# A two-layer streaming encoder on one core: where V's weights are scaled, how output weights are spaced, which engine forms V's left sums, and when layer 2's weight rows are loaded

## The chip, the cores and the metric

The kernel runs on one core of a Trainium2 chip. The core has five engines with a queue each: TensorE (PE) multiplies matrices into PSUM, VectorE (DVE) and ScalarE (ACT) work elementwise on SBUF and PSUM, GpSimd (POOL) works elementwise on SBUF, and SyncE (SP) issues the DMA transfers. Each queue runs in order; engines wait for each other through semaphores. The metric is the device time of one execution in microseconds; the median of several runs is compared.

## The reference

The input x has 2048 rows of 1024 floats. Layer A is a gated MLP, layer B an attention over chunks of 64 rows with K and V made once from the residual stream. All in float32:

```python
h = rms_norm(x, a_norm_g)
u, v, z = split(h @ w_in, 3)                       # each 2048 wide
u, v = gelu(u), layer_norm(gelu(v), ln_g, ln_b)
mixed = einsum('hts,bgshc->bgthc', masked(w_s), v in groups of 128 rows) + b_s
x = x + (u * mixed * silu(z)) @ w_out
k, v = split(rms_norm(x, kv_norm_g) @ w_kv, 2)     # 16 heads of 64
q, z = split(rms_norm(x, b_norm_g) @ w_qz, 2)
# each chunk of 64 rows attends to itself and the 8 chunks before it
p = softmax(q @ k.T / 8 + rel_bias[clipped distance])
x = x + ((p @ v) * silu(z)) @ w_b_out
return rms_norm(x, final_norm_g)
```

## The kernel before

**Split products.** Every large product is made of three matmuls of 128 x 512 (`mm3`, L99): a float32 operand is split into a high part (a rounded copy, made on ACT, L238) and a low part (the difference, made on DVE, L241). Left factors are called S, right factors T.

**Seven products in place of eight.** The products of layer A, the output product "o" and V's product "v" are blocked two by two, and each runs in seven passes, `PH = (1, 2, 6, 5, 7, 4, 3)`, with sums of blocks on the left and right and sums of results on the way out. A pass has eight steps (`NJ`), one for each pair of row blocks; the passes of n = 0, 1 (V of layer A), 2 to 5 (u and z), "o" and "v" make one list of steps, and `start[n, ph]` is the number of a pass's first step. A step has 12 matmuls, in "o" 24.

**The order by hand.** `run_steps` (L443) goes through the steps. In each it runs the events given for it with `at(s, f)`, then flushes what was put off with `later(k, f)` and issues the step's product and its eviction (`act`), prepares the left factor of the step three ahead (`prep`, `LOOK = 3`), and runs the weight work in `ts`. `later(1, f)` called from an event runs f in the same step, since the count is that of the last flush. Weight work is made by `make_t` (L250) and placed by `add_t` (L459): for each quarter (or half) q a load into a tile of the tag "raw" (four buffers), a combination of blocks on POOL (`pieces`, L243), and a finish, the split into T (ACT and DVE). Its offsets `(o, d)` mean step `start + o + d * q`.

**V's and layer 2's weights.** The norm gains are multiplied into the weights once: `load_scaled` (L149) loads a raw tile, multiplies on POOL (L157), and leaves the store of the scaled tile (L160) to the next call, by way of `deferred`. In "o" it is called eight times for V's weights (`wvs`, L888, steps nin + 20 and on, one every three) and three times for layer 2's first rows (L896), where `nin = start["o", 1]`. Layer 2's rows of the first chunk (t = 0) are scaled in place, in `one` (L1087), by `load_split` (L163), which loads, scales, splits and then feeds 24 matmuls; later chunks load the scaled rows from `wk3`.

**Left factors of "o".** `prep_out` (L802) loads blocks of y into the tag "A" (four buffers, `y_load`) and adds or subtracts them on DVE (L812, L815, L820).

**Rows between "o" and "v".** `row_load`, `row_norm` and `row_flip` (L908 to L945) load a finished row block, square it on ACT (into the PSUM tile that its transposes later use), take the power on POOL (L928), scale it on POOL (L930), transpose it on PE (L939) and store it.

**Left factors of "v".** `s7_of_v` (L992) makes s7 = a11 - a21 on POOL and a22 - s7 on DVE (L997), `s4_of_v` (L999) a third difference on POOL. s7 lies in one tile of the tag "hh", which the right factors of V's first pass use before it. `evict` (L346) takes the results out of PSUM; for V's first pass the copy is on DVE (L353), for "o" on ACT (L355). `done_vo` (L1002) splits the results of V (L1009 on ACT, L1010 on POOL).

**Startup.** `block_c` and `block_d` (L509, L519) make the left factors of the second row block of each pair; L724 to L728 place them among the norms of these blocks.

Of the kernel before, what the change touches and what calls it, by code (L numbers as in the profile page):

```python
# [9 lines left out]
F32 = mybir.dt.float32  # L10
# [7 lines left out]
P = 128  # L18
# [15 lines left out]
def trunk_kernel(  # L34
# [113 lines left out]

    def load_scaled(src, name, gain=None, keep=None):  # L149
        while deferred:  # L150
            deferred.pop(0)()
        raw = sh.tile([P, 1024], F32, tag="raw", name=f"raw_{name}", bufs=4)
        nc.sync.dma_start(raw[:], src)
        if gain is not None:
            k = gain.shape[1]
            r3 = raw[:].rearrange("p (k c) -> p k c", k=k)
            nc.gpsimd.tensor_tensor(  # L157
                r3, r3, gain.broadcast_to([P, k, 1024 // k]), op=ALU.mult
            )
            deferred.append(lambda: nc.sync.dma_start(keep, raw[:]))  # L160
        return raw
# [30 lines left out]
    with ExitStack() as actx:  # L192
# [153 lines left out]
        def evict(n, ph, j, ps, done, c22=None):  # L346
# [3 lines left out]
            if ph == 1:  # L350
                xa[n, j] = acc_tile(f"x{n}_{j}")
                if n == "v":
                    nc.vector.tensor_copy(xa[n, j][:], ps[:])  # L353
                else:
                    nc.scalar.copy(xa[n, j][:], ps[:])  # L355
# [103 lines left out]
        def add_t(ts, at, n, ph, src, nq, where, chain_of, offs):  # L459

            tops[n, ph], fs = make_t(n, ph, src, nq, where, chain_of)
            for f_, (o, d) in zip(fs, offs):
                for q in range(nq):
                    s = at + o + d * q
                    ts.setdefault(max(s, -LOOK), []).append(lambda f_=f_, q=q: f_(q))
# [258 lines left out]
        for j in range(NJ):  # L724
            e = j * 7 // 4
            norm_at(e - 1, e, block_b, j)
            at(e + 2, lambda j=j: block_c(j))
# [148 lines left out]
        for i, ph in enumerate(PH):  # L876
# [3 lines left out]
                6: ((-12, 2), (-11, 2), (-7, 1)),  # L880
                4: ((-14, 1), (-13, 1), (-7, 1)),
            }.get(ph, ((-9, 1), (-8, 1), (-7, 1)))
# [5 lines left out]
        for i, (r, c, q) in enumerate(wvs):  # L888
            g = kg[:, 4 * r + 2 * q : 4 * r + 2 * q + 2, :]
            at(  # L890
                nin + 20 + 3 * i,
                lambda r=r, c=c, q=q, g=g: load_scaled(
                    w_vv[r, c, q], f"bv{r}{c}{q}", g, wvs[r, c, q][:]
                ),
            )
        for c in range(3):  # L896
            at(nin + 43 + 2 * c, lambda c=c: load_scaled(*kqz_source(0, 0, c)))


# [16 lines left out]
        def row_norm(blk):  # L916
            xs = xn[blk]
            pool = ptrs[0] if blk // 2 % 2 else nxp[1]
            pt = pool.tile([P, KD, P], F32, tag="tr", name=f"tn{blk}")
            rs = [sm.tile([P, 1], F32, tag="rr", name=f"rn{blk}_{c}", bufs=6) for c in range(2)]  # L920
            for c in range(2):
                nc.scalar.activation(
                    pt[:, 4 * c : 4 * c + 4, :].rearrange("p a b -> p (a b)"), xs[c][:],
                    AF.Square, scale=1.0 / 32, accum_out=rs[c][:],
# [4 lines left out]
            for xt in xs:  # L929
                nc.gpsimd.tensor_scalar(xt[:], xt[:], r[:], 1.0, op0=mul, op1=mul)  # L930
            xn[blk] = xs, pt

        def row_flip(blk):
            t, b = divmod(blk, TB)
            xs, pt = xn.pop(blk)
# [19 lines left out]
        s7 = []  # L955
# [7 lines left out]
        def prep_v(ph, j):  # L963
# [13 lines left out]
            elif ph == 7:  # L977
                v = s7[0][:, j, :]
# [13 lines left out]
        def s7_of_v(j):  # L992
            if j == 0:
                s7.append(sh.tile([P, NJ, 512], F32, tag="hh", name="s7"))
            a, b = x_pair(1, j, "s")
            later(1, lambda: pieces(s7[0][:, j, :], sc[j][0], a, sub))
            later(2, lambda: tv(sc[j][0], b, s7[0][:, j, :], op=sub))  # L997

        def s4_of_v(j):  # L999
            pieces(sc[j][1], sc[j][1], sc[j][0], sub)  # L1000
# [39 lines left out]
        for j in range(NJ):  # L1040
# [4 lines left out]
            at(nv + 5 + 4 * j // 3, lambda j=j: s7_of_v(j))  # L1045
            at(start["v", 6] + 1 + j, lambda j=j: s4_of_v(j))
# [24 lines left out]
    with ExitStack() as bctx:  # L1071
# [15 lines left out]
        def one(t, p, c):  # L1087
            wh, wl = load_split(
                *kqz_source(t or p == 0, p, c)
            )  # L1090
# [424 lines left out]
```

## Time and profile before

| what | value |
|---|---|
| median of 3 runs | 2765.57 us (2763.31 to 2768.7) |
| the profiled execution, from start to end | 2760.59 us |
| its span, first to last instruction | 2758.8 us |
| granted PE clock over the span | 0.987 |
| DVE, ACT, POOL busy | 72%, 47%, 31% |
| DMA over the span | 655.33 MB, mean 238 GB/s |

A line of the profile names an instruction by its line in the kernel, engine, operation, and output <- inputs by tile names without their numbers. "So" is a left factor of "o", "Sv" of "v"; "Po" and "Pv" are their PSUM results; xv, yv, cv and xo are results being summed; "As" and "A" are blocks loaded for the left factors; "tn" holds transposes of normed rows. "SPq" is the DMA queue of SP. "PEld" is the load of weights into PE, which overlaps its matmuls. A matmul's time is a latency: in a full pipeline one starts every 0.23 us and takes 0.39. An arrow in a wait names who ended it.

### The profile page before, as it was taken

Reading aid. Unit: us, or ns where it says so; the run is one execution under the profiler, and the core shown is the slowest. Engines: PE = TensorE matmul, PEld = TensorE weight load, DVE = VectorE, ACT = ScalarE, POOL = GpSimd, SP = SyncE. Lnnn points to the kernel's source line nnn. Section 1 sums busy time; section 2 is a strip of 40 time slices with the busy share of each in tenths; the row PEclk is TensorE's granted clock in tenths of the full one; section 3 lists DMA queues with packets and bytes.
Section 4 is the critical chain, followed back from the end, with each engine's and each line's share of the span. In section 5 each row is a group of like instructions: output and inputs, shape, how many; then the busy total and the mean of one; then the engine's idle time right before and its main releaser. Section 6 shows DMA issues by size and latency. Waiting matters only on the chain.

```text
span 2758.8 us, 38718 instructions
## 1 busy us (share of the span) xinstructions
PE 2658.7 (96%) x13312; PEld 2212.1 (80%) x13312; DVE 1972.8 (72%) x3081; ACT 1300.1 (47%) x2266; POOL 844.3 (31%) x811
## 2 busy tenths in 40 slices
PE   8999999999999999989897999999999999999997
PEld 7788888888888888777676777878888888888886
DVE  5655666676666777856546857778888888878887
ACT  5422242433434343322452545655666566746663
POOL 3511124131321315335537555312221222212221
PEclk9999999999999999999999999999999999999999
DMA  7899999987868777767996787555556555555431
GB/s 285 297 325 340 316 330 328 322 304 236 330 225 301 290 272 288 258 222 272 320 293 199 256 297 249 179 178 159 166 161 207 153 152 157 174 166 165 141 123 61
DMA packets 265636, 655.33 MB, mean 238 GB/s; under 512 B 26465, under 2 KB 71521, under 8 KB 265441
## 3 DMA queue, kind: packets, MB, share of 16 engines
q1 hardware_dynamic: 265440, 652.86, 70.3%
q8 instruction: 106, 1.74, 0.3%
q14 instruction: 90, 0.73, 0.1%
HBM read 501.76 MB, written 140.51 MB: 233 GB/s over the span
## 4 chain that ended last, share of the span: by engine, by line
PE 68%; DVE 11%; DMA 8%; POOL 5%; issue 5%; ACT 2%; SPq 1%; POOLq 0%; DVEq 0%; ACTq 0%
PE P L100 9%; PE P L101 9%; PE P L102 9%; PE pj L100 5%; PE pj L101 5%; PE pj L102 5%; PE s L1187 4%; PE tp L1226 4%; PE pv L1253 3%; DMA A<-ytd 2%; PE bo L102 2%; PE bo L101 2%; PE bo L100 2%; DMA raw_b<-in_w_kqz 1%; DVE pt L1230 1%
## 5 line engine op out<-in xcount | busy, mean ns | idle before, releaser
L100 PE MATMUL P<-T,S 128*128 128x512 f32 x1248 | 497.2, 398 | 2.7 <-ACT S L238 1.7
L101 PE MATMUL P<-T,S 128*128 128x512 f32 x1248 | 488.4, 391 | 0.5 <-DVE T L241 0.5
L102 PE MATMUL P<-T,S 128*128 128x512 f32 x1248 | 488.7, 392 | 0.0
L1206 POOL TENSOR_SCALAR pr<-pr,sl 128x640 f32<-128x640 f32 (+4 forms) x256 | 208.3, 814 | 708.3 <-DVE sl L1205 655.5
L100 PE MATMUL pj<-hh_b,wh_b 128*128 128x512 f32 x768 | 314.5, 410 | 1.2 <-ACT hh_b L136 1.2
L101 PE MATMUL pj<-hl_b,wh_b 128*128 128x512 f32 x768 | 304.5, 396 | 1.1 <-DVE hl_b L137 1.1
L102 PE MATMUL pj<-hh_b,wl_b 128*128 128x512 f32 x768 | 302.8, 394 | 0.0
L102 PEld LDWEIGHTS P<-T,S 128*128 128x128 f32 x1248 | 235.5, 189 | 50.6
L100 PEld LDWEIGHTS P<-T,S 128*128 128x128 f32 x1248 | 235.8, 189 | 47.5 <-ACT S L238 1.9
L101 PEld LDWEIGHTS P<-T,S 128*128 128x128 f32 x1248 | 235.9, 189 | 44.9 <-DVE T L241 0.9
L1202 ACT ACTIVATE pr<-pr,nm 128x640 f32<-128x640 f32 (+4 forms) x256 | 195.6, 764 | 118.3 <-DVE nm L1195 111.0
L1230 DVE TENSOR_TENSOR pt<-tp,pt 128x640 fp32r<-128x640 f32 (+4 forms) x256 | 188.6, 737 | 58.9 <-ACT pt L1229 57.0
L1229 ACT CAST pt<-tp 128x640 fp32r<-128x640 f32 (+4 forms) x256 | 159.2, 622 | 135.9 <-PE tp L1226 134.5
L1195 DVE CUSTOM_DVE_ANT_0 pr<-s,bias 128x640 f32<-128x640 f32 (+4 forms) x256 | 188.0, 734 | 28.1 <-PE s L1187 23.3
L1226 PEld LDWEIGHTS tp<-ident,pr 128*128 128x128 f32 x1120 | 131.7, 140 | 54.6 <-POOL pr L1206 17.4
L1226 PE MATMUL tp<-ident,pr 128*128 128x128 f32 x1120 | 166.0, 274 | 8.5 <-POOL pr L1206 6.1
L102 PEld LDWEIGHTS pj<-hh_b,wl_b 128*128 128x128 f32 x768 | 145.0, 189 | 29.7
L100 PEld LDWEIGHTS pj<-hh_b,wh_b 128*128 128x128 f32 x768 | 145.2, 189 | 19.4 <-ACT hh_b L136 2.8
L101 PEld LDWEIGHTS pj<-hl_b,wh_b 128*128 128x128 f32 x768 | 145.9, 190 | 15.8 <-DVE hl_b L137 2.0
L1253 PE MATMUL pv<-pt,V 128*128 128x256 f32 x960 | 139.6, 285 | 0.0
L169 DVE TENSOR_TENSOR wl_b<-raw_b,wh_b 128x1024 fp32r<-128x1024 f32 x96 | 121.5, 1266 | 24.7 <-ACT wh_b L168 23.2
L168 ACT CAST wh_b<-raw_b 128x1024 fp32r<-128x1024 f32 x96 | 100.5, 1049 | 66.7 <-PE pj L101 37.6
(249 smaller groups left out, 5955.7 us busy)
## 6 DMA issues: line engine op xcount, KB each, us to landing
S<-hsd SPq DMA_DIRECT2D x288, 512.0 KB, 5.2
rw<-in_w_a SPq DMA_DIRECT2D x108, 512.0 KB, 6.0
raw_b<-wk SPq DMA_DIRECT2D x75, 512.0 KB, 4.0
A<-ytd SPq DMA_DIRECT2D x72, 512.0 KB, 5.4
hsd<-S SPq DMA_DIRECT2D x56, 512.0 KB, 3.9
V<-vhd SPq DMA_DIRECT2D x112, 256.0 KB, 4.3
rwo<-in_w_out SPq DMA_DIRECT2D x40, 512.0 KB, 5.0
bias<-reld SPq DMA_DIRECT2D x64, 320.0 KB, 3.0
```

The costliest lines, as they stand in the source:

```text
L100: mm(ps, lh, rh, start=first, stop=False)
L101: mm(ps, lh, rl, start=False, stop=False)
L102: mm(ps, ll, rh, start=False, stop=last)
L169: nc.vector.tensor_tensor(wl[:], raw[:], wh[:].bitcast(F32), op=ALU.subtract)
L1187: mm(ps[:, sg, :w], q[:, qb * P : (qb + 1) * P], kx[:, koff + sg * w : koff + (sg + 1) * w], start=i == 0, stop=i == 1,)
L1195: nc.vector.tensor_tensor_reduce(out=pr[:, c0:].rearrange("p (a b) -> p a b", a=nseg), in0=ps[:, :nseg, :w], in1=bias[:, c0:].rearrange("p ...
L1202: nc.scalar.activation(pr[:, c0:], pr[:, c0:], AF.Exp, scale=-1.0, bias=nm[:], accum_out=sl[:])
L1206: nc.gpsimd.tensor_scalar(pr[:, c0:], pr[:, c0:], sl[:], 1.0, op0=ALU.mult, op1=ALU.mult)
L1226: tpose(tp[:, b, :], pr[:, b * P : (b + 1) * P], ident[:])
L1229: nc.scalar.copy(oh, tp[:, b0:5, :])
L1230: nc.vector.tensor_tensor(pt[:, 1, b0 + qq : 5 + qq, cs], tp[:, b0:5, :], oh.bitcast(F32), op=ALU.subtract)
L1253: mm(po[:, 0, :], keys(i), pt[:, j, i, :], start=(t == 0 and j == 0 and i == blocks[0]), stop=(j == 1 and i == blocks[-1]),)
```

## The change

- **V's weights and layer 2's first rows** are loaded, scaled and stored in the u/z passes: eleven jobs, the first five in n = 5, the next five in n = 4, the last in n = 3, each three steps ahead of a pass. A function of its own, `scaled`, loads in the event, multiplies in the same step's flush and stores two steps later. The calls in "o" are gone.
- **The output weights' quarters** are two steps apart in every pass but the first, with a step each between load, combination and finish. `add_t` now goes quarter by quarter, so within one step the functions of an earlier quarter come first.
- **V's left sums**: s7 and the third difference are formed on DVE; s7 lies in eight tiles of the tag "acc"; s7 begins at nv + 2 in place of nv + 5 (`nv = start["v", 1]`). The copies of V's first pass out of PSUM go from DVE to ACT.
- **Row norms**: the squares are written to a bfloat16 SBUF tile, the scaling is on ACT and put off by `later(1)`, and the PSUM tile is taken in `row_flip`.
- **Layer 2 rows**: after each `load_split` in `one`, the raw tile of the next product (in the order 1, 0, 2 within a pair of heads, then the next pair, then the next chunk) is loaded and kept in `early`.
- **Startup**: all norms are placed before all `block_c` and `block_d`.

```diff
+    early = {}
+    def load_raw(src, name):
+        raw = sh.tile([P, 1024], F32, tag="raw", name=f"raw_{name}", bufs=4)
+        nc.sync.dma_start(raw[:], src)
+        return raw
     def load_scaled(src, name, gain=None, keep=None):
         while deferred:
             deferred.pop(0)()
-        raw = sh.tile([P, 1024], F32, tag="raw", name=f"raw_{name}", bufs=4)
-        nc.sync.dma_start(raw[:], src)
+        raw = early.pop(name, None) or load_raw(src, name)
...
                 xa[n, j] = acc_tile(f"x{n}_{j}")
-                if n == "v":
-                    nc.vector.tensor_copy(xa[n, j][:], ps[:])
-                else:
-                    nc.scalar.copy(xa[n, j][:], ps[:])
+                nc.scalar.copy(xa[n, j][:], ps[:])
...
-            for f_, (o, d) in zip(fs, offs):
-                for q in range(nq):
+            for q in range(nq):
+                for f_, (o, d) in zip(fs, offs):
                     s = at + o + d * q
...
             norm_at(e - 1, e, block_b, j)
+        for j in range(NJ):
+            e = j * 7 // 4
             at(e + 2, lambda j=j: block_c(j))
...
                 1: ((-11, 1), (-9, 1), (-8, 1)),
-                6: ((-12, 2), (-11, 2), (-7, 1)),
-                4: ((-14, 1), (-13, 1), (-7, 1)),
-            }.get(ph, ((-9, 1), (-8, 1), (-7, 1)))
+                6: ((-11, 2), (-10, 2), (-8, 2)),
+            }.get(ph, ((-10, 2), (-9, 2), (-8, 2)))
...
-        for i, (r, c, q) in enumerate(wvs):
-            g = kg[:, 4 * r + 2 * q : 4 * r + 2 * q + 2, :]
-            at(
-                nin + 20 + 3 * i,
-                lambda r=r, c=c, q=q, g=g: load_scaled(
-                    w_vv[r, c, q], f"bv{r}{c}{q}", g, wvs[r, c, q][:]
-                ),
-            )
-        for c in range(3):
-            at(nin + 43 + 2 * c, lambda c=c: load_scaled(*kqz_source(0, 0, c)))
+        def scaled(src, name, gain, keep):
+            raw = sh.tile([P, 1024], F32, tag="raw", name=f"raw_{name}", bufs=4)
+            nc.sync.dma_start(raw[:], src)
+            k = gain.shape[1]
+            r3 = raw[:].rearrange("p (k c) -> p k c", k=k)
+            later(1, lambda: nc.gpsimd.tensor_tensor(
+                r3, r3, gain.broadcast_to([P, k, 1024 // k]), op=mul
+            ))
+            later(3, lambda: nc.sync.dma_start(keep, raw[:]))
+        jobs = [
+            (w_vv[r, c, q], f"bv{r}{c}{q}", kg[:, 4 * r + 2 * q : 4 * r + 2 * q + 2, :],
+             wvs[r, c, q][:])
+            for r, c, q in wvs
+        ] + [kqz_source(0, 0, c) for c in range(3)]
+        for i, job in enumerate(jobs):
+            n, ph = 5 - i // 5, (1, 5, 7, 4, 3)[i % 5]
+            at(start[n, ph] - 3, lambda job=job: scaled(*job))
...
         def row_norm(blk):
             xs = xn[blk]
-            pool = ptrs[0] if blk // 2 % 2 else nxp[1]
-            pt = pool.tile([P, KD, P], F32, tag="tr", name=f"tn{blk}")
+            jk = nxp[0].tile([P, 2, 512], BF16, tag="xv", name=f"jn{blk}", bufs=4)
...
-            for xt in xs:
-                nc.gpsimd.tensor_scalar(xt[:], xt[:], r[:], 1.0, op0=mul, op1=mul)
-            xn[blk] = xs, pt
+            def scale():
+                for xt in xs:
+                    nc.scalar.mul(xt[:], xt[:], r[:])
+            later(1, scale)
...
         def s7_of_v(j):
-            if j == 0:
-                s7.append(sh.tile([P, NJ, 512], F32, tag="hh", name="s7"))
             a, b = x_pair(1, j, "s")
-            later(1, lambda: pieces(s7[0][:, j, :], sc[j][0], a, sub))
-            later(2, lambda: tv(sc[j][0], b, s7[0][:, j, :], op=sub))
+            s7[j] = acc_tile(f"s7_{j}")
+            later(1, lambda: tv(s7[j][:], sc[j][0], a, op=sub))
+            later(2, lambda: tv(sc[j][0], b, s7[j][:], op=sub))
         def s4_of_v(j):
-            pieces(sc[j][1], sc[j][1], sc[j][0], sub)
+            tv(sc[j][1], sc[j][1], sc[j][0], op=sub)
...
-            at(nv + 5 + 4 * j // 3, lambda j=j: s7_of_v(j))
-            at(start["v", 6] + 1 + j, lambda j=j: s4_of_v(j))
+            at(nv + 2 + 9 * j // 8, lambda j=j: s7_of_v(j))
+            at(start["v", 6] + 2 + j, lambda j=j: s4_of_v(j))
...
         def one(t, p, c):
-            wh, wl = load_split(
-                *kqz_source(t or p == 0, p, c)
-            )
+            def source(t, p, c):
+                src, _, *gain = kqz_source(t or p == 0, p, c)
+                return src, f"b{t}_{p}_{c}", *gain
+            wh, wl = load_split(*source(t, p, c))
+            i = 3 * (NPAIR * t + p) + (1, 0, 2).index(c) + 1
+            if i < 3 * NPAIR * NT:
+                nxt = i // 3 // NPAIR, i // 3 % NPAIR, (1, 0, 2)[i % 3]
+                early[f"b{nxt[0]}_{nxt[1]}_{nxt[2]}"] = load_raw(*source(*nxt)[:2])
```

More of the change, by code (lines that the diff above doesn't have):

```diff
@@ L922, in row_norm @@
                 nc.scalar.activation(
-                    pt[:, 4 * c : 4 * c + 4, :].rearrange("p a b -> p (a b)"), xs[c][:],
-                    AF.Square, scale=1.0 / 32, accum_out=rs[c][:],
+                    jk[:, c, :], xs[c][:], AF.Square, scale=1.0 / 32, accum_out=rs[c][:],
                 )
@@ L928, in row_norm @@
             nc.gpsimd.tensor_tensor(r[:], r[:], mhalf[:], op=ALU.pow)
-            for xt in xs:
-                nc.gpsimd.tensor_scalar(xt[:], xt[:], r[:], 1.0, op0=mul, op1=mul)
-            xn[blk] = xs, pt
+            def scale():
+                for xt in xs:
+                    nc.scalar.mul(xt[:], xt[:], r[:])
+            later(1, scale)
         def row_flip(blk):
             t, b = divmod(blk, TB)
-            xs, pt = xn.pop(blk)
+            xs = xn.pop(blk)
+            pool = ptrs[0] if blk // 2 % 2 else nxp[1]
+            pt = pool.tile([P, KD, P], F32, tag="tr", name=f"tn{blk}")
             for c, xt in enumerate(xs):
@@ L953, in x_load @@
             nc.sync.dma_start(v, xTd[t][:, ks, b * P : b * P + P])
-        s7 = []
+        s7 = {}
         def x_pair(r, j, nm):
@@ L977, in prep_v @@
             elif ph == 7:
-                v = s7[0][:, j, :]
+                v = s7.pop(j)[:]
             elif ph == 4:
```

## The prediction

> **What bounds the kernel now.** I read the page's engine line first, then windows over the stages, then the waits of TensorE (PE) stage by stage, and only then the timeline at the longest gaps.
>
> ```profile
> PE 2658.7 (96%) x13312; PEld 2212.1 (80%) x13312; DVE 1972.8 (72%) x3081; ACT 1300.1 (47%) x2266; POOL 844.3 (31%) x811
> ```
>
> PE is busy 96% of the span of 2758.8 us: about 100 us of idle time is all that an edit that leaves the matmuls alone can win, besides what PE loses to a lowered clock. Where that time lies is read from four windows: the u/z passes (400 to 1077), the output product "o" (1045.7 to 1405.4), V (1405.4 to 1598) and the first part of layer 2 (1598 to 1760). The columns are the length, each engine's busy time and instructions, the granted PE clock, the DMA share and GB/s.
>
> ```profile
> 400.00:1077.00 677.00, 674.99 (x3257) 563.74 (x3256) 477.74 (x564) 269.17 (x439) 194.50 (x106) 1.00 0.83 291
> 1045.70:1405.40 359.70, 329.25 (x1434) 263.84 (x1433) 228.85 (x252) 122.28 (x215) 160.93 (x100) 0.97 0.80 274
> 1405.40:1598.00 192.60, 170.39 (x730) 136.40 (x729) 127.39 (x146) 79.60 (x135) 116.89 (x81) 0.96 0.77 248
> 1598.00:1760.00 162.00, 150.80 (x775) 122.96 (x774) 107.07 (x255) 91.49 (x207) 76.29 (x113) 0.99 0.77 250
> ```
>
> The u/z passes lose 2.0 us in 677 (677 - 674.99). "o" loses 30.4 (359.70 - 329.25), V 22.2 (192.60 - 170.39) and early layer 2 11.2 (162 - 150.80). A granted clock of 0.97, 0.96 and 0.99 there takes at most another 10.8, 7.7 and 1.6 us (3%, 4%, 1% of the lengths). So these three stretches hold 64 us of idle time and up to 20 us of slow clock. What PE waits for, as total, times and longest, first in "o", then V, then layer 2:
>
> ```profile
> PE Po L102 <- DVE So L241: 18.8, 12, 4.0
> PE tn L939 <- ACT xo L942: 7.2, 3, 6.2
> PE Po L100 <- ACT So L238: 3.2, 3, 2.2
> PE tn L939 <- POOL bx L930: 1.2, 1, 1.2
> ...
> PE Pv L100 <- DVE cv L348: 7.3, 4, 3.7
> ...
> PE tn L939 <- POOL bx L930: 4.8, 3, 3.1
> PE Pv L100 <- DVE xv L348: 2.7, 2, 2.1
> PE Pv L100 <- ACT Sv L238: 2.0, 1, 2.0
> ...
> PE tp L1226 <- POOL pr L1206: 6.1, 4, 2.4
> PE s L1187 <- DMA Qh<-Qh: 4.4, 1, 4.4
> ```
>
> In "o" PE waits for left factors (So), in V for VectorE (DVE) to empty its PSUM tiles, in both for the transposes of the normed rows, and in layer 2 for the probabilities that POOL scales.
>
> **V's weights leave "o".** Here is how one of the long gaps in "o" comes about (timeline, start and duration, what the engine waited for in brackets):
>
> ```profile
> 1181.95 0.33 SPq L153 DMA_DIRECT2D raw_bv<-in_w_vv  x1
> 1185.52 1.90 POOL L157 TENSOR_TENSOR raw_bv<-raw_bv,kg 128x1024 f32<-128x1024 f32 x1 [3.60 <-DMA raw_bv<-in_w_vv]
> 1187.44 0.33 SPq L160 DMA_DIRECT2D wvs<-raw_bv  x1
> 1190.44 7.11 SPq L790 DMA_DIRECT2D A<-ytd  x3
> 1192.60 0.39 PE L100 MATMUL Po<-To_hh,So 128*128 128x512 f32 x1
> 1192.83 0.39 PE L101 MATMUL Po<-To_hl,So 128*128 128x512 f32 x1
> 1194.77 1.23 DVE L812 TENSOR_TENSOR A<-A,A 128x1024 f32<-128x1024 f32 x1 [16.95 <-DMA A<-ytd]
> 1197.25 0.50 PE L102 MATMUL Po<-To_hh,So 128*128 128x512 f32 x1 [4.04 <-DVE So L241]
> 1198.06 0.63 PE L102 MATMUL Po<-To_hh,So 128*128 128x512 f32 x1
> 1198.48 0.63 PE L100 MATMUL Po<-To_hh,So 128*128 128x512 f32 x1
> ...
> 1201.46 0.40 PE L101 MATMUL Po<-To_hl,So 128*128 128x512 f32 x1
> ...
> 1212.03 0.80 PE L102 MATMUL Po<-To_hh,So 128*128 128x512 f32 x1 [3.85 <-DVE So L241]
> ...
> 1284.33 0.80 PE L102 MATMUL Po<-To,So 128*128 128x512 f32 x1 [3.95 <-DVE So L241]
> ```
>
> SP issues V's raw weights at 1181.95, POOL scales them from 1185.52 when they have landed, and SP, which issues in order, stands at the store wvs until 1187.44; the loads A<-ytd come behind it at 1190.44, DVE has idled 16.95 us when they land, and PE stands 4.04 us. Afterwards matmuls start 0.42 us apart (1198.06, 1198.48) in place of 0.23 (1192.60, 1192.83). That lasts from 1198.06 to 1201.46, eight starts, so 8 x 0.20 = 1.6 us more: **a gap of 4 us costs 5.6**. Two more such gaps end at 1212.03 (3.85) and 1284.33 (3.95).
>
> The change moves all eight weight jobs, and the three loads of layer 2's first rows, into the u/z passes of n = 5, 4 and 3, one every eight steps; the load is issued three steps ahead of a product, POOL's multiply in the same step and the store two steps later. What goes from "o" is on POOL:
>
> ```profile
> L157 POOL TENSOR_TENSOR raw_bv<-raw_bv,kg 128x1024 f32<-128x1024 f32 x8 | 16.4, 2056 | 56.8 <-DMA raw_bv<-in_w_vv 45.6 <-DVE A L815 11.2
> ```
>
> 16.4 us of work and 45.6 us in which POOL stood for those loads, with combinations of the output weights and the sums with x behind it; and on SP eight loads, eight stores and the raw buffers that they held. Alongside, the quarters of the output weights come one every two steps (load, combine, finish at offsets -10, -9, -8, then -8, -7, -6 and so on), where most came one per step; so DVE's two products of weight splitting no longer fall into four successive steps. The last quarter is ready by step -2 in place of -4, and is used by the last quarter of the first product only; I cost that at nothing; a quarter late by one POOL instruction (2.06 us, the row above) in all seven passes would cost 14. Within a step the work now goes quarter by quarter in every pass, a change of place by one instruction, which I cost at nothing too. Of the 18.8 + 3.2 us that PE waits for So, three gaps make 4.04 + 3.85 + 3.95 = 11.8, with 1.6 of slow clock each 16.6. The first is the job's outright, the second stands in the same backlog 15 us later, the third, 72 us later, I ascribe by half: 5.6 + 5.5 + 2.8 = 13.9; for the nine small ones (22.0 - 11.8 = 10.2) I take 4. **"o" gains 18.** The bounds are -14 (late quarters, and the loads A<-ytd, four buffers for two per step, late by themselves) and 30.4 + 10.8 = 41.
>
> **What the jobs cost in u/z.** Eleven multiplies of about 2 us (22 us) join POOL's 194.50 us in 677, and the jobs' loads and stores are put in front of the left factors' loads on SP. The nearest row for an SP that stands in these passes:
>
> ```profile
> SPq L580 <- DVE vl L241: 74.7, 24, 9.8
> ```
>
> SP already stands there 24 times, up to 9.8 us at once, and PE loses 2.0 us in all; the left factors have six buffers, so they are five products ahead. A job's store waits for its load and multiply, within that 9.8. I take 2 us for all eleven. Bounds: nothing, and a 5.6 us gap for each, 62.
>
> **V's left sums on VectorE.** Before, each block's first sum runs on POOL, the second on DVE, the third on POOL, and each waits for the other engine:
>
> ```profile
> L997 DVE TENSOR_TENSOR sv<-As,s x8: 681/1746/1774, 1445.0 to 1487.2; 128x512 f32<-128x512 f32 x8
> L245 POOL TENSOR_TENSOR s<-sv,As 128x512 f32<-128x512 f32 x8 | 11.1, 1400 | 0.0
> L245 POOL TENSOR_TENSOR sv<-sv 128x512 f32<-128x512 f32 x8 | 11.9, 1490 | 7.1 <-DVE sv L997 7.1
> 1440.00:1480.00 40.00, 32.70 (x125) 25.53 (x124) 25.98 (x24) 12.93 (x20) 34.07 (x22) 0.89 0.67 211
> ```
>
> DVE's sum takes 681 ns at best and 1746 in the median, POOL's 1400 and 1490; in 1440 to 1480 POOL is busy 34.07 of 40 us and the clock is 0.89, which takes up to 4.4 us. There lie the 7.3 us of waiting for cv and the 2.0 for Sv behind it. After the change all three run on DVE without a handover, start three steps sooner (the tile no longer shares the buffer of the first weights), and 11.1 + 11.9 = 23 us leave POOL; DVE gains 16 sums and gives the eight copies out of PSUM of the first product to ScalarE (ACT). DVE was busy 127.39 of 192.60, so 16 x 0.68 = 11 us fit. **V gains 7.3 + 2.0 + 4 = 13**; bounds -11 (the sums hold up PE in full) and 22.2 + 7.7 = 30. A sum that is issued ahead of its load would hold DVE's queue, the evictions behind it too; three steps of factors are ready by then, so I cost it at nothing.
>
> A rule speaks against this edit: the Trainium skill's page "SBUF — State Buffer", section "Who interferes with whom", says that a DVE instruction with two SBUF inputs and a GpSimd instruction that reads SBUF block each other for their whole length, and these sums have two. The 1746 ns against 681 agrees. By it, the sums keep meeting POOL's work on vo, which stays; that is a rival below.
>
> **Row norms.** The squares' unused output goes to SBUF in place of PSUM, so the transposes' tile is taken two steps later, and the scaling goes from POOL to ACT:
>
> ```profile
> L930 POOL TENSOR_SCALAR bx<-bx,rn 128x512 f32<-128x512 f32 x32 | 27.8, 881 | 1.6
> L922 ACT ACTIVATE tn<-bx 128x512 f32<-128x512 f32 x32 | 19.2, 601 | 7.4 <-DMA bx<-x1d 6.1
> 1320.00:1440.00 120.00, 104.19 (x496) 82.82 (x497) 58.48 (x86) 65.58 (x137) 49.12 (x55) 0.96 0.98 309
> ```
>
> 32 scalings of 881 ns leave POOL; ACT, whose square of the same shape takes 601, gets about 32 x 0.6 = 19 us and the eight copies, 5 us, on top of 65.58 in 120. It also stands in order for POOL's power, which I put at 1 us for each of 16 rows: 106 of 120. The 1.2 + 4.8 us of waits for POOL's scaling go, but what is late next are the copies xo (7.2 now) and the splits behind a standing ACT. I take nothing; bounds +6.0 and -13 (the 7.2 doubled and 6 more).
>
> **Layer 2 rows one product ahead.** For the first chunk the rows are scaled on POOL, which stands for each load with the probabilities' scaling behind it:
>
> ```profile
> L157 POOL TENSOR_TENSOR raw_b<-raw_b,bg 128x1024 f32<-128x1024 f32 x16 | 31.8, 1990 | 30.6 <-DMA raw_b<-in_w_kqz 29.5 <-issue 1.0
> L157 POOL TENSOR_TENSOR raw_b<-raw_b,kg 128x1024 f32<-128x1024 f32 x8 | 15.6, 1952 | 15.7 <-DMA raw_b<-in_w_kqz 13.7 <-issue 2.0
> ```
>
> 29.5 + 13.7 us of standing. That is 1.8 us for each of the 24. With the raw tile loaded a product sooner (24 matmuls, at least 24 x 0.23 = 5.5 us), these waits are over before POOL comes to them, and PE's four waits for pr, 6.1 us, go: **6 gained**. The wait for Qh (4.4) stands behind other DMAs on SP, whose order the edit shuffles; I leave it. Bounds -4.4 (one more such wait) and 11.2 + 1.6 = 13. Later chunks load unscaled rows, and PE is not short of them: no gain; one of four raw buffers is taken longer.
>
> **First layer.** Norms now stand ahead of the splits in a step:
>
> ```profile
> PE t L392 <- DVE hb L494: 6.9, 2, 3.6
> ```
>
> Four of eight blocks change places by one instruction each; either sign, up to 3.6 us. I take nothing.
>
> **Sum.** 18 + 13 + 6 - 2 = 35 us. The profiled execution took 2760.59 us, 1.8 more than its span and 5.0 less than the median of the runs, 2765.57. 2760.6 - 35 = 2725.6 for an execution like it, 2730.6 as a median: **2731**.
>
> **Rivals.**
> - Sums still blocked: DVE's sums and splits meet vo on POOL as before at 1.75 us, the stall in V stays, 13 us fewer: 2744. For it: 681 against 1746 ns; against: 23 us of POOL work leave the same stretch. 0.14.
> - "o" bound by its own loads: A<-ytd has four buffers, two per step, and 4.3 us from its issue (1190.44) to DVE's sum (1194.77), so it stays late without the jobs; "o" gains 5 for 18: 2744. For it: the gap at 1284.33; against: the timeline of 1181 to 1197. 0.14.
> - Both of these and ACT late in the norms, or early loads that SP issues no sooner since it works in order: 35 - 13 - 13 - 6 = 3, 2763. 0.08.
> - Better: no gap stays long enough to lower the clock, so all 20 us of it come back in place of the 9 counted (3 gaps at 1.6 and 4 in V), and with POOL free 20 us of the smaller gaps go too: 35 + 11 + 20 = 66, 2700. For it: the slow starts follow a gap of 4 us; against: the smaller gaps have other releasers. 0.10. The Trainium skill's page "TensorE: Matmul & The Clock Gate", section "What's actually happening", bears on this rival: the clock halves after an idle window of about 3.4 us and is back after a busy one; the 3.4 us of slow starts from 1198.06 agree.
> - Slower: SP stands at each job's load (raw buffers full of the next pass's weights) and again at its store, more than the five products' lead allows, and the left factors come late in u/z. At 5.6 us a job, eleven make 62; it decides from the seventh job (7 x 5.6 = 39 over the 18 + 13 + 6 = 37 gained elsewhere); all eleven give 2765.6 + 62 - 37 = 2791. For it: exactly this happened in "o"; against: 2.0 us lost where SP stands 9.8. 0.12.
>
> My forecast keeps 0.42. What a measurement tells from no change is about 0.2%, 5.5 us. Faster: 0.42 + 0.14 + 0.14 + 0.10 = 0.80; same 0.08; slower 0.12. The range leaves out the slower case and half of the best: 2702 to 2766.
>
> **What would show it.** Right: in "o" idle time near 16 us and no gap of 4 us; V's wait for cv gone and a clock near 1 in its second product; no wait of tp for pr above 0.5 us early in layer 2; the u/z windows within 4 us of full. Wrong: gaps in u/z with releaser DMA S; ACT over 100 us of 120 during the row norms with PE behind xo; DVE sums still at 1.7 us with PE behind cv.

## The result and the profile after

The changed kernel took 2747.82 us (median of 4 runs, 2741.25 to 2748.59) beside 2767.14 us before (2763.31 to 2770.64): a ratio of 0.9925, 95% interval 0.9904 to 0.9946, or 19.3 us gained. The forecast was 2731 us with a range of 2702 to 2766; the direction was right and the time 17 us off. The profiled execution of the changed kernel took 2747.29 us, its span is 2745.5 us, 13.3 less than before.

The engine line of the page after, then four stretches of the windows (length, then busy time and instructions of PE, PEld, DVE, ACT, POOL, then clock, DMA share, GB/s). "o" now starts at 1056.1, V at 1416.6 and layer 2 at 1588.3.

```profile
PE 2655.2 (97%) x13312; PEld 2212.5 (81%) x13312; DVE 1983.3 (72%) x3089; ACT 1322.0 (48%) x2306; POOL 801.7 (29%) x763
```

```profile
400.00:1045.00 645.00, 637.77 (x3068) 531.57 (x3067) 452.56 (x532) 251.05 (x408) 195.21 (x104) 1.00 0.85 304
1056.10:1416.60 360.50, 327.60 (x1435) 264.83 (x1434) 229.28 (x255) 137.77 (x240) 127.35 (x70) 0.95 0.78 256
1416.60:1588.30 171.70, 163.66 (x727) 132.98 (x726) 128.19 (x153) 86.81 (x150) 81.44 (x52) 0.98 0.76 249
...
1320.00:1440.00 120.00, 94.78 (x429) 75.74 (x430) 54.93 (x78) 75.66 (x153) 21.70 (x20) 0.87 0.89 281
```

"o" is as long as before (360.50 against 359.70) and V, from its first matmul to the first of layer 2, 20.2 us shorter (171.7 against 191.9). The u/z passes now lose 7.2 us in 645. In the stretch of the row norms PE works 94.78 of 120 us at a clock of 0.87, before 104.19 at 0.96; POOL went from 49.12 to 21.70 there and ACT from 65.58 to 75.66.

What PE waits for after the change (total, times, longest), in u/z, "o", V and early layer 2:

```profile
PE mx L101 <- DVE vl L247: 4.7, 2, 2.4
...
PE tn L953 <- ACT xo L956: 14.9, 3, 9.5
PE tn L953 <- ACT bx L941: 8.1, 1, 8.1
PE Po L102 <- DVE So L247: 6.4, 6, 3.8
PE Po L100 <- ACT So L244: 3.4, 2, 2.9
...
PE Pv L100 <- DVE cv L354: 2.2, 1, 2.2
...
PE tp L1245 <- POOL pr L1225: 2.9, 2, 2.7
```

The waits for So fell from 18.8 + 3.2 to 6.4 + 3.4 us and those for cv from 7.3 to 2.2. In their place PE stands 14.9 + 8.1 us for transposes of the rows, of which 7.2 and 1.2 were there before. Here is ACT during that stand (timeline, start and duration):

```profile
1321.56 0.63 ACT L932 ACTIVATE jn<-bx 128x512 bf16<-128x512 f32 x1 [19.35 <-DMA bx<-x1d]
...
1325.15 1.33 ACT L941 ACTIVATE bx<-bx,rn 128x512 f32<-128x512 f32 x2 [1.72 <-POOL rn L937]
...
1330.25 1.33 ACT L941 ACTIVATE bx<-bx,rn 128x512 f32<-128x512 f32 x2 [1.44 <-POOL rn L937]
...
1335.90 1.33 ACT L941 ACTIVATE bx<-bx,rn 128x512 f32<-128x512 f32 x2 [0.40 <-POOL rn L937]
...
1337.65 0.57 ACT L956 COPY xo<-tn 128x512 f32<-128x512 f32 x1
...
1338.28 1.12 PE L953 MATMUL tn<-ident,bx 128*128 128x128 f32 x4 [9.53 <-ACT xo L956]
```

The first row's transposes are made at 1325.9, as soon as ACT has scaled it, but its copy out of PSUM, xo, starts at 1337.65: in ACT's queue it stands behind the squares and scalings of the next two rows, and those wait for POOL's power (1.44 and 0.40 us; the 1.72 us are the first row's own) and for loads (0.91 and 0.54 us). ACT is busy 75.66 of 120 us; it isn't full, it is in the wrong order for PE.

### The profile page after: what moved, and what is told of

Same layout as the page of the kernel before. It is cut to its first block, busy times and chain, and to the rows that moved or that the text cites. A ratio compares the mean times of both kernels' runs of the same rounds, so it can differ in the third digit from the quotient of the medians.

```text
span 2745.5 us, 38660 instructions
## 1 busy us (share of the span) xinstructions
PE 2655.2 (97%) x13312; PEld 2212.5 (81%) x13312; DVE 1983.3 (72%) x3089; ACT 1322.0 (48%) x2306; POOL 801.7 (29%) x763
## 4 chain that ended last, share of the span: by engine, by line
PE 40%; DVE 8%; DMA 7%; POOL 2%; issue 2%; ACT 2%; SPq 0%; DVEq 0%; POOLq 0%; ACTq 0%
PE pj L100 5%; PE pj L101 5%; PE pj L102 5%; PE s L1206 4%; PE tp L1245 4%; PE pv L1272 3%; PE bo L100 2%; PE bo L102 2%; PE bo L101 2%; DMA A<-ytd 1%; DMA bx<-x1d 1%; DMA rwo<-in_w_out 1%; DMA xr<-in_x 1%; PE Pv L100 1%; PE Pv L101 1%
## 5 line engine op out<-in xcount | busy, mean ns | idle before, releaser
L1245 PEld LDWEIGHTS tp<-ident,pr 128*128 128x128 f32 x1120 | 131.9, 140 | 50.4 <-issue 15.3
```

The lines of the kernel that those rows point to most:

```text
L1245: tpose(tp[:, b, :], pr[:, b * P : (b + 1) * P], ident[:])
```

## Experiments

Each run is timed beside the kernel before on the same chip; a ratio is to that kernel. The lengths of passes are read off each profile, from the first matmul of a pass to the first of the next; start("o") is the first matmul of "o". The executions of one kernel lie 4 to 17 us apart, so the lengths of one profile are read for the large differences and for what many profiles share. The profiled executions of e1 and e12 took 7.4 and 7.6 us less than their medians, that of e4 7.2 us more.

| run | median us (runs) | ratio, 95% interval | start("o") | o: pass 2 | o: 5 + 7 | o: 4 + 3 | V |
|---|---|---|---|---|---|---|---|
| before | 2767.14 (4) | 1 | 1045.7 | 48.7 | 110.5 | 110.5 | 191.9 |
| after | 2747.82 (4) | 0.9925, 0.9904 to 0.9946 | 1056.1 | 54.7 | 89.3 | 126.1 | 171.7 |
| e1_pool_scale | 2743.04 (6) | 0.9913, 0.9894 to 0.9933 | 1047.1 | 52.3 | 89.5 | 118.9 | 173.0 |
| e2_norms_old | 2735.55 (6) | 0.9891, 0.9874 to 0.9908 | 1054.7 | 51.6 | 89.4 | 111.4 | 175.3 |
| e11_norms_only | 2768.21 (12) | 1.0008, 0.9994 to 1.0022 | 1047.6 | 48.1 | 108.7 | 119.2 | 183.7 |
| e3_ph6_old | 2739.9 (6) | 0.9899, 0.9881 to 0.9916 | 1053.5 | 51.2 | 88.6 | 122.1 | 171.0 |
| e5_offs_old | 2738.21 (4) | 0.9892, 0.9876 to 0.9908 | 1053.1 | 49.1 | 88.6 | 122.8 | 174.2 |
| e4_jobs_in_o | 2765.91 (12) | 0.9994, 0.9981 to 1.0007 | 1045.4 | 54.8 | 104.2 | 124.0 | 183.5 |
| e10_jobs_only | 2750.73 (6) | 0.9927, 0.9908 to 0.9947 | 1050.8 | 51.8 | 90.8 | 112.8 | 188.9 |
| e6_v_only | 2755.66 (6) | 0.9959, 0.9944 to 0.9974 | 1047.1 | 49.4 | 106.7 | 114.4 | 182.7 |
| e7_early_only | 2766.62 (12) | 0.9995, 0.9984 to 1.0007 | 1046.6 | 50.3 | 111.4 | 114.1 | 193.0 |
| e9_three_parts | 2730.92 (4) | 0.9868, 0.985 to 0.9887 | 1056.5 | 47.5 | 88.0 | 113.0 | 171.6 |
| e8_rows_later | 2731.8 (4) | 0.9862, 0.9843 to 0.9881 | 1050.9 | 48.5 | 89.5 | 112.5 | 176.2 |
| e12_moved | 2737.17 (4) | 0.9894, 0.9877 to 0.991 | 1052.8 | 50.0 | 87.8 | 113.3 | 172.8 |

**Row norms.** Theory A: the rows' gaps come from ACT's queue. Rivals: rows that land late whichever engine scales them (B), or the PSUM tile (C).

```diff
 e1: the changed kernel with
-            def scale():
-                for xt in xs:
-                    nc.scalar.mul(xt[:], xt[:], r[:])
-            later(1, scale)
+            for xt in xs:
+                nc.gpsimd.tensor_scalar(xt[:], xt[:], r[:], 1.0, op0=mul, op1=mul)
 e2: the changed kernel with row_norm and row_flip as before
 e11: the kernel before with row_norm and row_flip as changed
```

> The changed kernel with the rows' scaling back on POOL; everything else as changed. Theory A (ScalarE's queue): passes 4 and 3 of "o" grew from 59.7 + 50.8 = 110.5 us to 67.8 + 58.3 = 126.1 because squares, scalings and copies xo stand behind one another on ScalarE. Then they come back to 108 to 113 us, no gap of 8 us is left there, and the time is 2748 - 15 = 2733. Rival B (late rows): TensorE merely comes sooner to rows whose loads land late on SP, whichever engine scales them. Then the two passes stay at 122 to 128 us and the time at 2744 to 2750.

> The changed kernel with the rows' norms as before altogether: squares into the PSUM tile of the transposes, scaling on POOL. Theory A: the same as with the scaling alone put back, 2733 within 4 us, since the squares' place costs nothing. Rival C (the PSUM tile's early take was the cost): passes 4 and 3 of "o" come out longer than in that run by 5 us or more, time 2738 to 2745. Rival B (late rows): 2744 to 2750.

> The kernel before with the new row norms alone (squares into SBUF, scaling on ScalarE, the PSUM tile taken later). Theory A (ScalarE's queue costs 12 us wherever TensorE stands): passes 4 and 3 of "o" from 110.5 to 120 us or more, time 2780. Rival J (it costs only where TensorE has come sooner to rows that land late): passes 4 and 3 within 4 us of 110.5, time 2764 to 2772.

With the scaling alone back on POOL (e1) passes 4 and 3 came to 118.9 us, between the two theories, and the median to 2743: its interval overlaps that of the changed kernel. With the whole norm as before (e2) they came to 111.4 us and the median to 2735.55, 12.3 below the changed kernel; the two intervals only just touch (0.9904 and 0.9908). What PE waits for in "o", first with the scaling on POOL:

```profile
PE tn L950 <- ACT xo L953: 10.6, 2, 7.9
PE tn L950 <- POOL bx L940: 6.8, 1, 6.8
```

and with the whole norm as before:

```profile
PE tn L950 <- POOL bx L941: 8.0, 1, 8.0
...
PE tn L950 <- ACT xo L953: 3.3, 3, 1.5
```

The wait for xo goes only when the squares, too, are where they were. ACT's queue shows why. In e1 the first row is transposed at 1313.75, and its copy has to wait for the squares of the third row, which stand ahead of it in the queue and wait for their loads (3.96 and then 1.13 us):

```profile
1320.28 0.63 ACT L932 ACTIVATE jn<-bx 128x512 bf16<-128x512 f32 x1 [3.96 <-DMA bx<-x1d]
...
1323.79 0.57 ACT L953 COPY xo<-tn 128x512 f32<-128x512 f32 x1
```

In e2 it is transposed at 1319.93, and the third row's squares come after the copies:

```profile
1323.55 0.57 ACT L953 COPY xo<-tn 128x512 f32<-128x512 f32 x1
...
1326.30 0.60 ACT L933 ACTIVATE tn<-bx 128x512 f32<-128x512 f32 x1 [0.26 <-DMA bx<-x1d]
```

So theory A holds for ACT's order, with more of it in the squares than I had put there. That the order comes from the PSUM tile, which the squares can't have before an earlier row has been copied out of it, is argued from the tile's reuse. How the 12 us split between squares and scaling is open, since the intervals of e1 and e2 overlap. B is right about the rest: a first wait of 7 to 9 us for a scaled row stays in all of these.

The norms alone on the kernel before (e11) fit neither expectation: passes 4 and 3 grew by 8.7 us, as A said, and the time didn't change, as J said. V, 8.2 us shorter, gave it back. Its waits in V:

```profile
PE Pv L100 <- DVE cv L348: 5.7, 3, 3.7
...
PE tn L942 <- ACT bx L930: 2.3, 4, 1.2
```

The waits of tn for the rows are half of the 4.8 us before and those for cv are 1.6 us shorter, which is half of the 8.2; that POOL, rid of its scalings, holds V up less is the likely reason. The table has one rule for all its rows: where the norms are the new ones, passes 4 and 3 take 119.2 to 126.1 us (five profiles), where they are the old ones 110.5 to 114.4 (eight). Some 10 us are the price in "o". V returns 8 of it where POOL makes V's sums; with the sums on DVE it is 171.7 us long with the new norms and 175.3 (e2) or 171.6 (e9) with the old, so little comes back.

**The quarters' spacing.**

```diff
 e3: the changed kernel with
-                6: ((-11, 2), (-10, 2), (-8, 2)),
+                6: ((-12, 2), (-11, 2), (-7, 1)),
 e5: the changed kernel with all offsets as before
```

> The changed kernel with the offsets of the output weights' second pass (number 6) as before: loads at -12, combinations at -11, finishes from -7. Theory D (the finish comes two steps behind the combination in place of four, so ScalarE's split of the weights waits for POOL with the left factors' splits behind it): the second product of "o" (pass 2) goes back from 54.7 to about 48.7 us, its gaps of 2.9 and 3.8 us go, and the time is 2748 - 6 = 2742. Rival E (something else holds POOL or ScalarE there, such as the layer's last sums): 54 to 55 us again, 2748.

> The changed kernel with the offsets of all output weights' quarters as before, jobs and all else as changed. Theory F (only the jobs' leaving took the gaps of 4 us out of "o"; the spacing earns nothing): passes 5 and 7 stay at 89 to 92 us, pass 2 is near 51 us, and the time is 2740, as with the offsets of the second pass alone put back (2739.9). Rival H (the spacing carries part of the gain): passes 5, 7 and 4 grow together by 4 us or more against that run, time 2744 or more.

In the table of offsets the passes go by their numbers; the weights of pass 6 are made while pass 2 runs. Both runs took 8 to 10 us off the median (2739.9, 2738.21); their intervals overlap that of the changed kernel, that of e5 by little. Pass 2 went from 54.7 to 51.2 and 49.1 us, passes 5 and 7 from 89.3 to 88.6 in both. Rival H falls: the spacing carried none of the gain. What ACT waits for while pass 2 runs (window 1085 to 1145), with the new spacing:

```profile
ACT To L244 <- POOL cho L251: 22.6, 3, 10.3
ACT So L244 <- DMA A<-ytd: 9.5, 2, 7.6
...
ACT So L244 <- PE Po L102: 1.6, 1, 1.6
```

and with the old:

```profile
ACT To L244 <- POOL cho L251: 20.3, 3, 7.5
ACT So L244 <- PE Po L102: 14.1, 6, 3.6
```

With the old offsets ACT waits 14.1 us for PE, which means that it is ahead of it; with the new ones 1.6. In total ACT waits for POOL about as long with both; what differs is how long at once, and when. With the new offsets the split To of the last quarter comes two steps later than with the old. It waits 10.3 us, until 1134.82, for POOL's combination, which itself stood 7.7 us for its load; five splits So stand behind it, and PE waits 2.94 us for one of them, until 1136.44. The next gap, 3.83 us, ends with a split So on DVE that took 2.83 us beside a combination on POOL, where others took 0.68. So theory D holds for its mechanism, though not by "two steps in place of four": with the old offsets the four splits came four, three, two and one steps behind their combinations. Pass 2 came back by 3.5 to 5.6 us (in e3 one gap of 3.7 us is left in it), and of the 8 to 10 us of the medians the rest isn't in one place that I can name.

**The jobs.**

```diff
 e4: the changed kernel with the calls of load_scaled in "o", as before
 e10: the kernel before with `scaled` and its eleven jobs in u/z
```

> The changed kernel with the eleven weight jobs back in "o", as before, and all else as changed. Theory F (the jobs made the long gaps in "o", and cost 8 us where they are now): passes 5 and 7 of "o" go from 43.5 + 45.8 = 89.3 back to about 110 us, "o" starts near 1048 us in place of 1056, and the time is 2748 + 21 - 8 = 2761. Rival G (the quarters' spacing took the gaps away): passes 5 and 7 stay at 89 to 94 us, "o" starts near 1048, and the time is about 2740.

> The kernel before with the eleven weight jobs moved into u/z alone. Theory F alone: passes 5 and 7 of "o" from 110.5 to 87 to 91 us, 5 to 9 us lost in passes 4.5, 5.6 and 5.5 of u/z, time 2767.9 - 18 = 2750. Rival J (a TensorE that comes 14 us sooner to pass 4 finds the rows late): passes 4 and 3 of "o" with the first of V grow by 8 us or more against 146.1, time 2756 or more.

Back in "o" the jobs cost 18.1 us (2765.91 against 2747.82), and their move alone gains 17.7 (ratio 0.9927). Passes 5 and 7 take 104.2 and 106.7 to 111.4 us in the four other profiles with jobs in "o" (the kernel before among them), and 87.8 to 90.8 in the nine with jobs in u/z. With the jobs back the waits in "o" are there again, under all the new spacing (e4):

```profile
PE Po L102 <- DVE So L247: 16.0, 8, 4.1
...
PE Po L100 <- ACT So L244: 10.9, 3, 4.8
```

F holds and G falls. Rival J of e10 is met by half: passes 4 and 3 with the first of V took 155.7 us, 9.6 more than before, but the time is F's. The price in u/z is the start of "o": 1047.1 to 1056.5 us in the nine profiles with the jobs there, mean 1052.8; 1045.4 to 1047.6 in the five without, mean 1046.5. So the jobs cost 6.3 us in u/z, from 0 to 10 in single executions. SP's waits in the changed kernel from 740 to 1056 show how:

```profile
SPq L583 <- DVE vl L247: 29.5, 6, 9.4
SPq L900 <- POOL raw_bv L897: 8.3, 4, 3.3
SPq L894 <- DMA wvs<-raw_bv: 7.1, 2, 3.8
...
SPq L270 <- DMA wvs<-raw_bv: 5.6, 2, 3.4
SPq L270 <- DMA wk<-raw_b: 5.4, 2, 3.2
```

L900 is the job's store, which waits for its multiply and load; L894 the job's load and L270 the weights' load, which wait for a raw buffer until the store before has ended. Behind them stand the mixing loads va (L583). SP comes to these later: it stood there for 39.3 us before and 29.5 now. PE waits 4.7 us for vl; in the profiles with jobs in u/z these waits come to 2 to 6 us (0.5 in e12), in the five without to 0.7 at most. The left factors, whose lateness I had feared, are not late: no wait of PE for one appears from 400 us to the start of "o".

**V's sums.**

```diff
 e6: the kernel before with s7_of_v, s4_of_v, their steps and the copies of V's first pass as changed
```

> The kernel before with V's left sums on VectorE alone (seven difference in eight tiles, the copies of V's first pass on ScalarE, the new steps). Theory of the forecast: the handovers between POOL and VectorE held V; passes 6 and 5 of V go from 34.0 + 29.4 to 44 to 48 us and the time from 2767.7 to about 2750 (13 forecast, 20 by the trace of the changed kernel). Rival (sums still blocked, or the gain came from weights that are scaled earlier): the sums still take 1.75 us, V keeps 180 us or more of its 192.6, time 2762 or more.

2755.66, a gain of 12.3 us (ratio 0.9959): the forecast's 13, not the 20 of the changed kernel's V. The three sums in this run, on DVE (minimum, median and maximum, in ns):

```profile
L992 DVE TENSOR_TENSOR s<-sv,As x8: 680/684/2847, 1418.3 to 1465.4; 128x512 f32<-128x512 f32 x8
L993 DVE TENSOR_TENSOR sv<-As,s x8: 678/687/1186, 1419.0 to 1466.6; 128x512 f32<-128x512 f32 x8
L996 DVE TENSOR_TENSOR sv<-sv x8: 678/692/1778, 1447.4 to 1474.6; 128x512 f32<-128x512 f32 x8
```

and in the changed kernel:

```profile
L1009 DVE TENSOR_TENSOR s<-sv,As x8: 677/684/692, 1432.8 to 1466.8; 128x512 f32<-128x512 f32 x8
...
L1013 DVE TENSOR_TENSOR sv<-sv x8: 681/684/1780, 1435.7 to 1472.2; 128x512 f32<-128x512 f32 x8
```

The rival of blocked sums falls in both: no median is near 1.75 us. The long ones (over 1 us) are 4 of 24 in e6 and 3 of 24 in the changed kernel, where before they were 5 of DVE's 8, and each of them ran beside a two-input sum on POOL. Passes 6 and 5 of V took 44.9 us, as the theory had it, but V as a whole 182.7, as the rival had it, since pass 2 grew from 27.7 to 33.4. What is late there (e6, waits in V):

```profile
PE Pv L100 <- ACT xv L352: 5.3, 2, 3.2
...
PE Pv L100 <- DVE cv L348: 0.7, 1, 0.7
```

The wait for cv fell from 7.3 to 0.7 us, and two for the copies of the first pass, 5.3 us in all, came in with them on ACT, both in pass 2.

**Layer 2 rows.**

```diff
 e7: the kernel before with `early`, `load_raw` and the loads in `one` as changed
```

> The kernel before with the layer 2 rows loaded one product ahead alone. Theory: POOL no longer stands 1.8 us for each of 24 rows, the waits of tp for pr shrink from 6.1 us to under 3, and the time goes from 2767.7 to 2762 (6 forecast) or 2764 (4 by the trace of the changed kernel). Rival (SP works in order, so the loads come no sooner, or Qh comes later by what is gained): 2766 to 2769, and POOL still stands over 1 us for each row.

2766.62, ratio 0.9995: no difference. POOL's multiplies in the 162 us of early layer 2 before (busy, mean ns, then idle time in front of them):

```profile
L157 POOL TENSOR_TENSOR raw_b<-raw_b,bg 128x1024 f32<-128x1024 f32 x12 | 23.4, 1952 | 21.0 <-DMA raw_b<-in_w_kqz 19.9 <-issue 1.0
L157 POOL TENSOR_TENSOR raw_b<-raw_b,kg 128x1024 f32<-128x1024 f32 x6 | 11.4, 1897 | 13.7 <-DMA raw_b<-in_w_kqz 11.7 <-issue 2.0
```

and with early loads:

```profile
L163 POOL TENSOR_TENSOR raw_b<-raw_b,bg 128x1024 f32<-128x1024 f32 x12 | 24.2, 2018 | 18.6 <-DMA raw_b<-in_w_kqz 18.6
L163 POOL TENSOR_TENSOR raw_b<-raw_b,kg 128x1024 f32<-128x1024 f32 x6 | 11.4, 1899 | 15.4 <-DMA raw_b<-in_w_kqz 15.4
```

POOL stands 34.0 us for loads with them, 31.6 without. PE's waits for pr went from 6.1 to 3.6 us, the one for Qh from 4.4 to 5.8. One row, traced from SP's issue to POOL, shows that the lead didn't grow. Before:

```profile
1674.44 0.33 SPq L153 DMA_DIRECT2D raw_b<-in_w_kqz  x1
...
1679.94 1.90 POOL L157 TENSOR_TENSOR raw_b<-raw_b,kg 128x1024 f32<-128x1024 f32 x1 [4.18 <-DMA raw_b<-in_w_kqz]
```

with early loads:

```profile
1684.04 0.55 SPq L153 DMA_DIRECT2D raw_b<-in_w_kqz  x1
...
1689.38 1.90 POOL L163 TENSOR_TENSOR raw_b<-raw_b,kg 128x1024 f32<-128x1024 f32 x1 [4.00 <-DMA raw_b<-in_w_kqz]
```

5.5 us and 5.3 us from issue to multiply; over all 24 rows the medians are 5.6 and 5.3. On the queues the multiply follows its load as closely as before. Why the lead of a product in the program isn't one on the queues was not tried.

**The parts together, and two attempts at the rows.**

```diff
 e9: the changed kernel with the norms and all offsets as before
 e8: the changed kernel with the norms and pass 6's offsets as before, and
-                at(s_ + 1, lambda blk=blk: row_norm(blk))
-                at(s_ + 3, lambda blk=blk: row_flip(blk))
-            at(nv + 2 + 9 * j // 8, lambda j=j: s7_of_v(j))
+                at(s_ + 2, lambda blk=blk: row_norm(blk))
+                at(s_ + 4, lambda blk=blk: row_flip(blk))
+            at(nv + 3 + 9 * j // 8, lambda j=j: s7_of_v(j))
 e12: as e9, with row_load at s_ + 1, row_norm at s_ + 3, row_flip at s_ + 5, s7_of_v at nv + 4, and
-            n, ph = 5 - i // 5, (1, 5, 7, 4, 3)[i % 5]
+            n, ph = 5 - i // 5, (1, 2, 7, 4, 3)[i % 5]
```

> The kernel before with the three parts to which the forecast gave a gain (jobs in u/z, V's sums on VectorE, layer 2 rows early; the order of the startup as changed too), while the rows' norms and the quarters' offsets are as before. Theory I (norms and offsets each took their own time away, 12 and 10 us): 2748 - 12 - 10 = 2726, below the forecast's 2731. Rival J (both hurt through the same late rows between "o" and V, so putting both back gives no more than one): 2733 to 2738, with tn waiting for bx 8 us or more at the start of pass 4.

> The changed kernel with three things put right at once: the rows' norms as before (POOL scales, squares into PSUM), the second output pass's offsets as before, and each row block's norm and transposes, and V's left sums behind them, one step later. Theory (rows' loads land late against a TensorE that now comes sooner; each edit takes its own gap away): passes 4 and 3 of "o" and 1 of V together from 155 us (61.1 + 50.3 + 43.8 with the norms as before) to 145 or less, no wait of tn for bx above 3 us, time 2735.5 - 3 - 8 = 2725. Rival (the gaps move by a step, or V's first pass starves for rows): 2733 to 2740.

> The kernel of the three parts (jobs, V's sums, early layer 2 rows) with two moves: the jobs of a pass 5 sit at pass 2, where the mixing loads come every four steps in place of three, and rows are loaded one step, normed and transposed two steps later, V's left sums two steps later. Theory K (in u/z the loss of 8 us comes from a job between mixing loads on SP's queue; at the row blocks TensorE and ScalarE stand only because rows are asked for before they have landed): "o" starts at 1046 to 1050 us in place of 1054.1, pass 4 of "o" goes from 61.5 to 54 us or less, no wait of tn for bx above 3 us, time 2731 - 5 - 6 = 2720. Rival L (any place of a job in u/z costs the same, and the rows' gap moves along with the rows): "o" starts at 1052 or later, passes 4, 3 and V's 1 stay at 150 us or more together, 2729 or more.

Without the norms' edit and the spacing the kernel takes 2730.92 us (ratio 0.9868, 0.985 to 0.9887), 16.9 below the changed kernel. The two cures alone were worth 12.3 and 9.6, 21.9 together; so they would overlap by 5, which is within the scatter: the time lies between I (2726) and J (2733 and up), and its interval, 2727 to 2737, takes in much of J and ends 1 us short of I. That the two edits together cost time is clear, since it ends below that of the changed kernel (0.9887 and 0.9904). What PE still waits for in "o" there:

```profile
PE tn L951 <- POOL bx L942: 9.4, 1, 9.4
```

The one long wait is the first row block of pass 4, whose load ACT awaits for 20.11 us:

```profile
1312.45 0.60 ACT L934 ACTIVATE tn<-bx 128x512 f32<-128x512 f32 x1 [20.11 <-DMA bx<-x1d]
```

SP's queue shows where the row is. SP stands 5.7 us at the store of a sum do, until 1305.03, since that sum on POOL waits 4.75 us for its load xr; the store of a row block xo follows at 1305.45, and the row's load, which reads it back, is issued when that store has landed, at 1308.11; ACT's square starts at 1312.45.

Asking for it later doesn't help. With rows one step later (e8, 2731.8) passes 4 and 3 with the first of V take 155.2 us, as long as in e2, and the waits in "o" are these:

```profile
PE Po L100 <- ACT So L244: 7.0, 2, 6.4
PE tn L950 <- POOL bx L941: 5.1, 1, 5.1
```

In e12, later by another step, they are 7.0 (longest 6.4) and 7.0 us, and the time is 2737.17. ACT stands at the first square with the splits So behind it, wherever its step is: the row itself isn't there. Pass 4 did come down to 53.4 us in e12, as theory K had it, but pass 3 grew to 59.9 from 51.5 in e9. The other move failed too: with the job at pass 2 the wait for vl went (0.5 us), one for x grew to 4.4 us (2.2 in e9), and "o" started at 1052.8 (1056.5 in e9). Theory K falls on both counts; L stands, though the three passes together are 149.2 us and not its 150.

## Why the prediction was right in direction and 17 us off

- **What bounds the kernel now**: right for two of the three stretches: in e9 "o" is 337.1 us long in place of 359.7 and V 171.6 in place of 191.9. Nothing was won in early layer 2.
- **V's weights leave "o"** (18 gained): the mechanism is shown by e4 and e10 from both sides, and passes 5 and 7 gave 19.7 us with the jobs alone. The third gap, which I ascribed by half, was the jobs' in full: the longest wait left in these passes in e10 is 1.8 us. The small gaps were twelve (12 + 3 - 3), not nine; the 10.2 us are right.
- In the same part, **the spacing, costed at nothing, is a step that failed**. The bound counted a quarter late by one POOL instruction, 2.06 us; here ACT's split To waited up to 10.3 us with So behind it, and pass 2 lost up to 5.6 us. Undoing the spacing gained 9.6 us by the medians, at the edge of what the runs can tell, and together with the norms 16.9, clear of it.
- **What the jobs cost in u/z** (2): under-sized; 6.3 us on average, up to 10. The jobs don't come one every eight steps throughout: passes 2 and 6 have none. I set SP's waits against the five products' lead of the left factors; the transfers behind SP without such a lead are the mixing loads, two buffers deep.
- **V's left sums on VectorE** (13): right alone (12.3), with some luck in the terms. The waits for cv and Sv went as counted (9.3 to 0.7 us); those for xv and yv on DVE also fell, from 8.1 to 1.0, which I hadn't counted, and the copies on ACT brought 5.3 that I had at nothing. The rule of the Trainium skill's page "SBUF — State Buffer", section "Who interferes with whom", and the trace agree on single sums (three third differences of 1765 to 1780 ns in the changed kernel, each beside a sum on POOL, and five near 684). The stall that it would have kept doesn't come; that this is because POOL has less to do in V (81.44 us in place of 116.89) is argued.
- **Row norms** (0, bounds +6.0 and -13): the step that failed by most. I named what would be late, the copies xo behind a standing ACT, and then took nothing; undoing them gained 12.3 us, close to the bound of 13. I weighed how full ACT is (at most 106 of 120); it was busy only 75.66 and late all the same.
- **Layer 2 rows one product ahead** (6): wrong. The gain is 0; the lead that it needed didn't come about, POOL stands as long as before, and the waits for pr fell by 2.5 us where 6.1 were to go. From layer 2 on the changed kernel's profile is 4 us shorter (1157.1 against 1161.4); that was not the edit's, since e9, which has it too, takes 1164.1.
- **First layer** (0): no run tells it from nothing. In e4, which has the new order and no jobs in u/z, "o" starts at 1045.4, and at 1045.7 to 1047.6 in the four kernels with the old.
- **The sum**: the three parts that I gave a gain took 37.5 us (2768.39 to 2730.92), forecast 18 + 13 + 6 - 2 = 35. That the number is met is partly luck: alone they measured 17.7, 12.3 and about 1, 31.4 in all. The other 6 are within the scatter of three runs, but the profiles have them in V: alone the jobs shorten it by 3.0 us and the sums by 9.2, together by 20.3. Pass 2 of V takes 33.0 us with the jobs alone, where PE waits 6.6 us at once for cv, and 33.4 with V's sums alone, where it waits for xv; it takes 22.4 with both. What in V needs both wasn't taken apart further. The two edits that I took as free cost 16.9.
- **What would show it**: the changed kernel has none of the signs of being right. Idle time in "o" is 32.9 us (16 expected) with gaps up to 9.5, cv is late by 2.2, the clock in V's second product is 0.93, the waits for pr are 2.9 us, and the u/z passes lose 7.2. e9 has the first: 15.3 us idle in "o". Of the signs of being wrong, PE behind xo came, but with ACT far from full.

## What to carry to other kernels

Work moved to an engine with time to spare is not free if that engine's queue also holds what the bottleneck waits for: look at what will stand behind each moved instruction, and behind the wait that it brings along, not at the engine's share of busy time. Where an edit is costed at nothing because two effects might cancel, carry its bad bound as a likely case. And undo the parts of a change one by one: here two of its parts gave back nearly half of what two others had gained, and the kernel without them is the faster one.

## What was not expected of the hardware

- Two waits of 8.06 and 9.53 us within 12.4 us stand in a stretch of 120 us whose granted clock is 0.87 (0.96 before); passes 4 and 3 grew by 15.6 us, part of it slow matmuls (from 1339.62 to 1341.75 they start 0.43 us apart in place of 0.23).
- A destination that nobody reads seems to matter: with the squares' unused output in SBUF (e1) or in PSUM (e2), and the scaling on POOL both times, the same two passes took 118.9 or 111.4 us. This is one profile of each.
